# First output projection: two weight blocks kept together and taken row tile by row tile, the norm of each tile taken apart into two steps

## The chip, the cores and the metric

The kernel runs on one core of a Trainium2 chip. The metric is the device time of one execution in microseconds (us). A core has TensorE (PE in the profile) for matrix products and transposes, VectorE (DVE), ScalarE (ACT), GpSimd (POOL) and SyncE (SP), which issues most of the loads. Each engine takes its instructions strictly in the order of the program.

## The reference, cut to what matters

One decoder layer runs over a prompt of 1024 tokens and over a sample group of 8 sequences with 8 new tokens each (64 rows), with 512 past positions of each in paged caches. The model width is 1024, the inner width of the feed-forward part 2816.

```
xn  = RMSNorm(x);  z = xn @ W_in
x   = x + [ RG-LRU | gated conv | forgetting attention | differential attention ] @ W_out
x   = x + (silu(RMSNorm(x) @ W_gate) * (RMSNorm(x) @ W_up)) @ W_down
y   = RMSNorm(x)
```

The change touches the end of the second line and the norm that begins the third, for the first half of the prompt (512 tokens, four row tiles of 128).

## The kernel before, in words

**Products.** All inputs are float32. A factor is held as a high part (`whi`, `xTh`) in a reduced float32 format and a low part (`wlo`, `xTl`, what is left over), and a product takes three matmuls: L94, L95 and L96. A weight block is loaded into one of **three `raw` buffers** (L310, L312). ACT then makes the high part of a quarter of it (L325) and DVE or GpSimd the low part (L326); the pairs stand in a **ring of eight**, so two blocks' worth of them can be there at a time. `W.load_to` and `W.split_to` run ahead of the products while `W.ahead` is on.

**First output projection** (`w_out_items(0, ...)`, L1593). W_out is cut into four column blocks n of 256. For each block, four row tiles t of 128 tokens are taken, each with 24 matmuls of 256 columns (8 blocks of the inner dimension by three). DVE adds the result to the residual `acc[t]` (L1608). All of block 0 comes first, then 1, 2 and 3.

**Second norm** (`norm2_items`, `norm_T`). For each tile: ACT squares and sums `acc[t]` (L430) into a scratch tile; `rsqrt_col` makes the reciprocal root in eight small operations on DVE (L432, L122 to L125); DVE scales by it and by the gain (L442) into the scratch tile; PE transposes it in eight steps (L449); ACT and DVE make the high and low parts (L451, L452). The scratch tile and the gain come from the same ring of three `raw` buffers as the weight blocks. The transposed tiles are new (`xT_tiles`).

**Attention of the samples** (`sample_items`). For each group of sequences: transposes of the gathered key pages (`spgk`, L1421), scores (L1436), a softmax on DVE and ACT (L1469 to L1479), transposes of the probabilities (L1490, L1493), products with the new and the gathered values (L1504, L1509), and a selection (L1519, L1523). After the last group follow a norm on DVE (L1539 to L1545) and two transposes (L1548).

**What sets the order.** The program is a list of items with estimated costs; `merge(a, b, frac)` interleaves two lists so that b is used up when `frac` of a's cost is. A list scheduler then orders each engine's instructions. Before, the output projection is merged with the first 60% (`P3_SMP`) of the sample attention, the four norms with the rest. Then come the loads of the prompt's second attention pass (`att1_open`) and the gate and up products of the feed-forward part, merged with that attention (scores at L1057). The first gate/up block is taken in two halves of 256 tokens (a gate half needs norm tiles 0 and 1, the other 2 and 3), the later ones over all 512.

Of the kernel before, what the change touches and what calls it, by code (L numbers as in the profile page):

```python
# [12 lines left out]
OP = mybir.AluOpType  # L13
# [29 lines left out]
P3_SMP = 0.6  # L43
# [5 lines left out]
NP_F = 8  # L49
# [4 lines left out]
WO_HEAD = 24  # L54
# [10 lines left out]
def hybrid_step(ctx, tc, I, C, O):  # L65
    nc = tc.nc
# [308 lines left out]
    W = WStream()  # L375
    widx = {}
# [46 lines left out]
    def gload(pool, src, eng=None):  # L423
        g = big(pool, "ng", 1)
        (eng or nc.sync).dma_start(g, dap(src, 0, [[0, 128], [1, D]]))
        return g
# [7 lines left out]
        (rsqrt_act if act else rsqrt_col)(y[:R], ms[:R], nrm, nm + "rs")  # L434
        return y

    st_x = {}

    def norm_T(pool, x, gb, R, xh, xl, c0, act=False):
        xs = big(pool, "nxs", 2)[:R]  # L440
        y = rstd_of(x, xs, R, "n", act)
        st_x["x"] = nc.vector.scalar_tensor_tensor(xs, x, y[:R], gb[:R], op0=OP.mult, op1=OP.mult)  # L442
        kn = 512 // R
        for kk in range(8 // kn):
            pt = bank("t")
            pv = pt.rearrange("p (k r) -> p k r", r=R)
            for i in range(kn):
                k = kk * kn + i
                nc.tensor.transpose(pv[:, i, :], xs[:, k * 128:(k + 1) * 128], ident[:R, :R])  # L449
            ks = slice(kk * kn, (kk + 1) * kn)  # L450
            nc.scalar.activation(xh[:, ks, c0:c0 + R], pv, AF.Copy)  # L451
            nc.vector.tensor_tensor(xl[:, ks, c0:c0 + R], pv, xh[:, ks, c0:c0 + R].bitcast(F32), op=OP.subtract)  # L452
        if R == 64:
            nc.vector.tensor_copy(xh[:, :, c0 + 64:c0 + 128], xl[:, :, c0:c0 + 64].bitcast(F32))

    def xT_tiles(pool, smp):
        xh = pool.tile([128, 8, 640 if smp else 512], F32R, name="xTh")
# [794 lines left out]
    def merge(a, b, frac=1.0):  # L1252

        r = []
        ca = sum(x[0] for x in a) * frac or 1
        cb = sum(x[0] for x in b) or 1
        i = j = 0
        xa = xb = 0.0
        while i < len(a) or j < len(b):
            if j >= len(b) or (i < len(a) and xa / ca <= xb / cb):  # L1260
                xa += a[i][0]
                r.append(a[i])
                i += 1
            else:
                xb += b[j][0]
                r.append(b[j])
                j += 1
        return r
# [322 lines left out]
                nc.sync.dma_start(xl[:, k, HALF:576].bitcast(F32), yD[k][0][1][:, HALF:576])  # L1591

    def w_out_items(hf, e):  # L1593
        items = []

        def f(n, t, c, kind):
            def mm(pt, k):
                wh, wl = wget("wo", hf, n)(k)
                yh, yl = e["xh"], e["xl"]
                if kind == "p":  # L1600
                    mm3(pt[:, :256], yh[:, k, c], yl[:, k, c], wh, wl, k == 0, k == 7)
                else:
                    nc.tensor.matmul(pt[:, :256], lhsT=yh[:, k, c], rhs=wh, start=k == 0, stop=False)
                    nc.tensor.matmul(pt[:, :256], lhsT=yh[:, k, c], rhs=wl, start=False, stop=k == 7)

            def end(pt):
                a = e["acc"][t][:, n * 256:(n + 1) * 256]
                nc.vector.tensor_tensor(a, a, pt[:, :256], op=OP.add)  # L1608
            r = []
            contract(r, (24 if kind == "p" else 16) * 256 * 0.417, ("wo", hf, n), 4, mm, end)  # L1610
            return r
        for n in range(4):
            r = [f(n, t, c, kind) for t, c, kind in tok_tiles(hf)]
            if hf == 0 and n == 0:
                items += sum((x[:3] for x in r[:3]), []) + sum((x[3:] for x in r[:3]), [])
                r = r[3:]
            items += sum(r, [])
        return items

    def fold_sample(a):  # L1620
        tm = wp.tile([128, RAWW], F32, name="raw", bufs=3)[:64, :D]
# [251 lines left out]
    def norm2_items(hf, e):  # L1873
# [14 lines left out]
            return g  # L1888
        return [(900, f(t)) for t in range(4 + hf)]

    def final_items(hf, e):
        st = {}

        def ends(ch):

            def g():
                a = e["acc"][3]
                if ch == 0:
                    o = st[3] = st["o"][:, 3]
                    ss = st["ss", 3] = nrm.tile([128, 4], F32, name="fs4")  # L1900
                    nc.scalar.activation(o[:, 0:512], a[:, 0:512], AF.Square, scale=256.0, accum_out=ss[:, 0:1])
                    nc.vector.tensor_scalar(ss[:, 3:4], ss[:, 0:1], EPS * 2.0 ** 26, None, op0=OP.add)
                    nc.vector.tensor_tensor(o[:, 0:512], a[:, 0:512], st["g"][:, 0:512], op=OP.mult)
                    return
                o, ss = st[3], st["ss", 3]
                w = slice(256 + ch * 256, 512 + ch * 256)
                nc.scalar.activation(o[:, w], a[:, w], AF.Square, scale=256.0, accum_out=ss[:, ch:ch + 1])
                if ch == 1:
                    return
                ms = nrm.tile([128, 1], F32, name="fms", bufs=5)  # L1910
                nc.vector.tensor_scalar(ms, ss[:, 3:4], ss[:, 1:2], ss[:, 2:3], op0=OP.add, op1=OP.add)
                y = nrm.tile([128, 1], F32, name="fry", bufs=5)
                rsqrt_act(y, ms, nrm, "frs")
                dst = O["y_prompt"][0, hf * HALF + 384:hf * HALF + 512, :]
                nc.vector.scalar_tensor_tensor(o[:, 512:], a[:, 512:], y, st["g"][:, 512:], op0=OP.mult, op1=OP.mult)
                nc.scalar.activation(o[:, 0:512], o[:, 0:512], AF.Copy, scale=y)
                nc.scalar.dma_start(dst[:, 0:512], o[:, 0:512])
                nc.sync.dma_start(dst[:, 512:], o[:, 512:])
            return g

        def f(t, ch):
            if hf and t == 3:
                return ends(ch)
            R = 128 if t < 4 else 64

            def square(a, h):
                nc.scalar.activation(st[t][:, h * 512:(h + 1) * 512], a[:R, h * 512:(h + 1) * 512], AF.Square,
                                     scale=256.0, accum_out=st["ss", t][:R, h:h + 1])

            def g():  # L1930
                a = e["acc"][t]
                if "g" not in st:
                    st["g"] = gload(None, I["norm_final_g"])
                    st["o"] = E2[0]["xp"].tile([128, 4, D], F32, name="fo", tag="xTh")
                    st["s"] = E2[0]["xp"].tile([128, 4, D], F32, name="fos", tag="xTl")
                if ch == 0:
                    st[t] = (st["o"][:, t] if t < 4 else st["s"][:, 0])[:R]
                    st["ss", t] = nrm.tile([128, 2], F32, name="fss", bufs=5)
                    if t < 4:
                        square(a, 0)  # L1940
                    return
                if t == 4:
                    fold_sample(a)
                    square(a, 0)
                square(a, 1)
                o, ss = st[t], st["ss", t]
                ms = nrm.tile([128, 1], F32, name="fms", bufs=5)
                nc.vector.tensor_scalar(ms[:R], ss[:R, 0:1], ss[:R, 1:2], EPS * 2.0 ** 26, op0=OP.add, op1=OP.add)
                y = nrm.tile([128, 1], F32, name="fry", bufs=5)
                (rsqrt_act if hf and t in (0, 1, 2, 3) else rsqrt_col)(y[:R], ms[:R], nrm, "frs")  # L1950
                pool = t in (FIN_POOL[:2] if hf else FIN_POOL)
                if pool:
                    nc.scalar.activation(o, a[:R], AF.Copy, scale=y[:R])
                    nc.gpsimd.tensor_tensor(o, o, st["g"][:R], op=OP.mult)
                dst = O["y_prompt"][0, hf * HALF + t * 128:hf * HALF + (t + 1) * 128, :] if t < 4 else \
                    O["y_sample"].rearrange("s t d -> (s t) d")
                if not pool:
                    nc.vector.scalar_tensor_tensor(o, a[:R], y[:R], st["g"][:R], op0=OP.mult, op1=OP.mult)
                nc.sync.dma_start(dst, o)
            return g  # L1960
        return f
# [12 lines left out]
    def do(f):  # L1974
        return [(0, f)]

    E1 = [{}, {}]
    E2 = [{}, {}]
# [118 lines left out]
    prog = do(head)  # L2097
# [5 lines left out]
    n = len(lg0)  # L2103
# [7 lines left out]
    k = len(G0["lg1"] + G0["fq"] + G0["fk"]) + len(F0["lg"])  # L2111
# [10 lines left out]
    SM_ITEMS = sample_items(SM)  # L2122
# [3 lines left out]
    n = NP_F  # L2126
# [11 lines left out]
    head, mid = block_split(ffn0, [("gu", 0, P3B - 1)])  # L2138
    mid, tail = block_split(mid, [("gu", 0, P4_SPLIT)])
    smp = SM_ITEMS[3:]  # L2140
    k = int(len(smp) * P3_SMP)
    wo = w_out_items(0, E2[0])
    prog += SM_ITEMS[:3] + wo[:WO_HEAD] + merge(wo[WO_HEAD:], smp[:k]) + merge(norm2_items(0, E2[0]), smp[k:]) + do(att1_open)
    prog += merge(head, att_items(A1, 1), P3_FRAC)
    prog += do(p3_b) + mid + do(p4_open) + w_out_items(1, E2[1])
    prog += merge(tail, norm2_items(1, E2[1]), 0.8)
# [92 lines left out]
```

## Time and profile before

| | |
|---|---|
| median of 3 runs | 1379.26 us (1373.75 to 1382.87) |
| profiled execution, its own time | 1379.24 us |
| span of the profiled execution | 1376.9 us |
| mean granted clock of TensorE | 0.991 of 2.4 GHz |
| last output-projection product of the stage | starts at 436.73 us |
| first gate product | starts at 453.57 us |

All positions are microseconds from the start of the span. "Busy" is the time in which an engine has an instruction running; the granted clock is 1.00 at 2.4 GHz and 0.50 at 1.2 GHz. A row of the timeline may stand for several equal instructions in a row: "x4" with a busy time for all four. A float32 product outside L94 to L96 shows as two records for each matmul. Behind a row, in brackets, stands the idle time of the engine ahead of it and what ended it.

### The profile page before, as it was taken

The page shows a single profiled execution, that of the slowest core. Times are in us where ns is not written, and L with a number is a line of the kernel's source. Part 1 is how long each engine was busy: PE and PEld are TensorE (multiplying, and loading weights), DVE is VectorE, ACT ScalarE, POOL GpSimd, SP SyncE. Part 2 cuts the span into 40 slices and gives each one's busy share as a digit, 9 for nine tenths or more (in the row PEclk, how much of TensorE's full clock was granted, in tenths as well). Part 3 has the DMA queues.
Part 4 walks back from the last instruction along what each step waited for, and adds up shares of the span by engine and source line. Part 5 has one row for each costly group of instructions (what it writes and reads, how often), then busy time and mean ns, then how long its engine had stood idle before and what let it go on. Part 6 is the DMA issues. An engine that isn't in the chain of part 4 may idle for free.

```text
span 1376.9 us, 23077 instructions
## 1 busy us (share of the span) xinstructions
PE 1345.7 (98%) x8477; PEld 1181.9 (86%) x8477; DVE 1060.9 (77%) x2699; ACT 675.6 (49%) x1326; POOL 126.7 (9%) x154
## 2 busy tenths in 40 slices
PE   9899998999999999999999999999999999999997
PEld 7799896878876688888888999997999999999996
DVE  6676377788556568899979988547998888888885
ACT  6575466756333258755544444324533444444454
POOL 3001012302243011000000000000200000000001
PEclk9999999999999999999999999999999999999999
DMA  8566438666994366444236433611624333333311
GB/s 260 175 194 205 132 125 266 205 201 222 343 333 142 108 216 217 139 138 123 77 115 196 125 92 93 191 47 62 197 63 123 93 92 92 93 92 93 93 47 69
DMA packets 202866, 202.65 MB, mean 147 GB/s; under 512 B 16529, under 2 KB 165549, under 8 KB 202626
## 3 DMA queue, kind: packets, MB, share of 16 engines
q1 hardware_dynamic: 189568, 168.60, 40.2%
q0 software_dynamic: 7328, 25.11, 5.0%
q10 hardware_dynamic: 5858, 7.47, 1.5%
q8 instruction: 67, 1.10, 0.3%
q14 instruction: 45, 0.37, 0.1%
HBM read 170.56 MB, written 32.29 MB: 147 GB/s over the span
## 4 chain that ended last, share of the span: by engine, by line
PE 81%; DVE 6%; ACT 6%; DMA 5%; issue 1%; SPq 0%; ACTq 0%; POOL 0%; DVEq 0%
PE pb_mm L94 11%; PE pb_mm L95 10%; PE pb_mm L96 10%; PE pb_mm L1743 8%; PE pb_s L1743 5%; PE pb_t L1743 5%; PE pb_t L94 3%; PE pb_t L95 2%; PE pb_t L96 2%; PE pb_o L1743 2%; PE pb_s L96 2%; PE pb_s L95 2%; PE pb_s L94 2%; PE pb_o L1161 2%; PE pb_t L1141 2%; DMA raw<-in_w_in_dram 2%
## 5 line engine op out<-in xcount | busy, mean ns | idle before, releaser
L325 ACT ACTIVATE whi<-raw 128x512 fp32r<-128x512 f32 (+1 forms) x409 | 251.8, 629 | 350.9 <-PE pb_mm L96 75.5
L326 DVE TENSOR_TENSOR wlo<-raw,whi 128x512 fp32r<-128x512 f32 (+1 forms) x405 | 275.8, 692 | 70.5 <-ACT whi L325 60.6
L94 PE MATMUL pb_mm<-xTh,whi 128*128 128x512 f32 (+2 forms) x536 | 192.3, 359 | 0.8 <-ACT whi L325 0.8
L95 PE MATMUL pb_mm<-xTl,whi 128*128 128x512 f32 (+2 forms) x536 | 191.1, 357 | 0.3 <-DVE xTl L452 0.3
L96 PE MATMUL pb_mm<-xTh,wlo 128*128 128x512 f32 (+2 forms) x536 | 190.6, 356 | 0.3 <-DVE wlo L326 0.3
L96 PEld LDWEIGHTS pb_mm<-xTh,wlo 128*128 128x128 f32 x536 | 101.0, 188 | 13.7 <-issue 1.6
L94 PEld LDWEIGHTS pb_mm<-xTh,whi 128*128 128x128 f32 x536 | 101.3, 189 | 12.7 <-ACT whi L325 1.1
L95 PEld LDWEIGHTS pb_mm<-xTl,whi 128*128 128x128 f32 x536 | 101.2, 189 | 10.8 <-DVE xTl L452 0.5
L94 PE MATMUL pb_mm<-whi,xTh 128*128 128x256 f32 (+1 forms) x312 | 91.1, 292 | 0.0
L1099 ACT ACTIVATE aP<-aP,anm 128x128 f32<-128x128 f32 (+7 forms) x96 | 74.0, 772 | 34.5 <-DVE anm L1097 32.2
L95 PE MATMUL pb_mm<-wlo,xTh 128*128 128x256 f32 (+1 forms) x312 | 88.3, 283 | 0.2 <-POOL wlo L326 0.2
L96 PE MATMUL pb_mm<-whi,xTl 128*128 128x256 f32 (+1 forms) x312 | 88.2, 283 | 0.0
L1829 DVE TENSOR_TENSOR acc<-acc,pb_mm 128x512 f32<-128x512 f32 (+1 forms) x95 | 64.4, 678 | 15.1 <-PE pb_mm L96 13.2
L94 PE MATMUL pb_mm<-whi,hTh 128*128 128x512 f32 (+1 forms) x179 | 70.7, 395 | 0.3 <-ACT hTh L1803 0.3
L96 PE MATMUL pb_mm<-whi,hTl 128*128 128x512 f32 (+1 forms) x179 | 70.6, 394 | 0.0
L95 PE MATMUL pb_mm<-wlo,hTh 128*128 128x512 f32 (+1 forms) x179 | 70.3, 393 | 0.0
L94 PEld LDWEIGHTS pb_mm<-whi,xTh 128*128 128x128 f32 x312 | 59.0, 189 | 5.0 <-issue 4.2
L95 PEld LDWEIGHTS pb_mm<-wlo,xTh 128*128 128x128 f32 x312 | 59.0, 189 | 0.8 <-POOL wlo L326 0.4
L96 PEld LDWEIGHTS pb_mm<-whi,xTl 128*128 128x128 f32 x312 | 58.9, 189 | 0.6 <-issue 0.4
L1743 PE MATMUL pb_mm<-xTh,whi 128*128 128x288 f32 (+1 forms) x184 | 53.7, 292 | 0.0
L1743 PE MATMUL pb_mm<-xTh,wlo 128*128 128x288 f32 (+1 forms) x184 | 53.6, 292 | 0.0
L1743 PE MATMUL pb_mm<-xTl,whi 128*128 128x288 f32 (+1 forms) x184 | 53.6, 292 | 0.0
(623 smaller groups left out, 3778.3 us busy)
## 6 DMA issues: line engine op xcount, KB each, us to landing
raw<-in_w_gate_dram SPq DMA_DIRECT2D x44, 512.0 KB
raw<-in_w_up_dram SPq DMA_DIRECT2D x44, 512.0 KB
raw<-in_w_down_dram SPq DMA_DIRECT2D x22, 1024.0 KB
raw<-in_w_in_dram SPq DMA_DIRECT2D x12, 1024.0 KB
raw<-in_w_in_dram SPq DMA_DIRECT2D x16, 512.0 KB
raw<-in_w_out_dram SPq DMA_DIRECT2D x8, 1024.0 KB
akt<-fkD SPq DMA_DIRECT2D x24, 256.0 KB
akt<-dkD SPq DMA_DIRECT2D x48, 128.0 KB
```

Of the source, the lines that this page charges most:

```text
L94: kp(nc.tensor.matmul(out, lhsT=lh, rhs=rh, start=first, stop=False))
L95: kp(nc.tensor.matmul(out, lhsT=lh, rhs=rl, start=False, stop=False))
L96: kp(nc.tensor.matmul(out, lhsT=ll, rhs=rh, start=False, stop=last))
L325: i1 = nc.scalar.activation(hi, s, AF.Copy)
L326: i2 = (nc.gpsimd if pool else nc.vector).tensor_tensor(lo, s, hi.bitcast(F32), op=OP.subtract)
L1099: nc.scalar.activation(dst[:, :ln], dst[:, :ln], AF.Exp, bias=nmx, accum_out=sm)
L1141: nc.tensor.transpose(pt[:, o:o + 128], P[ti][:, kb * 128:(kb + 1) * 128], ident)
L1161: nc.tensor.matmul(po[:, q0:q0 + n], lhsT=v[:, kb, :], rhs=a[:, o:o + n], start=kb == 0 and i == 0, stop=kb >= nkb - 2 and i == 1, skip_gr ...
L1743: nc.tensor.matmul(pt, lhsT=w[:, k], rhs=x[:, k], start=first and k == 0 and i == 0, stop=k == 3 and i == 2, skip_group_check=True)
L1829: nc.vector.tensor_tensor(a, a, pt, op=OP.add)
```

## The change

Weight blocks 0 and 1 of the output projection stay as they were. Blocks 2 and 3 are now taken together, row tile by row tile: for each tile the products of block 2, then of block 3, then the first step of its norm (`norm_a`: square and sum, reciprocal root, scale). The second step of the tile before (`norm_b`: transposes and copies) follows. Splitting ahead is off in this part; the four quarters of the first gate/up block are split in it by hand, between the last tile's products of block 2 and of block 3. All of the sample attention is merged with this list. The transposed tiles are written into the same `xh`, `xl` that held the projection's input. The second step of tile 3 comes after the first 16 items of the gate and up products (the first half of the first block).

```
-    def norm_T(pool, x, gb, R, xh, xl, c0, act=False):
+    def norm_a(pool, x, gb, R, act=False):
         xs = big(pool, "nxs", 2)[:R]
         y = rstd_of(x, xs, R, "n", act)
...
+        return xs
+    def norm_b(xs, R, xh, xl, c0):
...
-            items += sum(r, [])
-        return items
+            if hf == 0 and n >= 2:
+                late.append(r)
+            else:
+                items += sum(r, [])
+        return (items, late) if hf == 0 else items
...
-    k = int(len(smp) * P3_SMP)
-    wo = w_out_items(0, E2[0])
-    prog += SM_ITEMS[:3] + wo[:WO_HEAD] + merge(wo[WO_HEAD:], smp[:k]) + merge(norm2_items(0, E2[0]), smp[k:]) + do(att1_open)
+    wo, (w2, w3) = w_out_items(0, E2[0])
+    nrm2 = norm2_steps(E2[0])
+
+    def split_next():
+        i = widx["gu", 0, 0]
+        W.split_to(i, 4)
+
+    rows = do(lambda: setattr(W, "ahead", False))
+    for t in range(4):
+        rows += w2[t] + (do(split_next) if t == 3 else []) + w3[t] + do(nrm2[t][0])
+        if t:
+            rows.append((430, nrm2[t - 1][1]))
+    prog += SM_ITEMS[:3] + wo[:WO_HEAD] + merge(wo[WO_HEAD:] + rows, smp) + do(lambda: setattr(W, "ahead", True))
+    prog += head[:2 * NP_F] + [(430, nrm2[3][1])] + do(att1_open)
+    head = head[2 * NP_F:]
     prog += merge(head, att_items(A1, 1), P3_FRAC)
```

The added lines move what follows: L449, L451, L452 of before are L452, L454, L455 after, and the lines of the sample attention stand six further down (L1421 is L1427, L1436 is L1442, L1548 is L1554).

On **ACT**, around the first square of the second norm (L430; `acc0` is the residual of tile 0; the `whi` rows ahead of it in the first piece are the high parts of the first gate/up block), before:

```order
L325 ACTIVATE whi_5516<-raw_5225 128x512
L325 ACTIVATE whi_5520<-raw_5225 128x512
L325 ACTIVATE whi_5524<-raw_5225 128x512
L325 ACTIVATE whi_5528<-raw_5225 128x512
L1423 ACTIVATE skT_5540<-pb_t_5541 128x512
L430 ACTIVATE raw_5768,nss_5769<-acc0_4829 128x1024
```

The same place after (`raw_5273` is the first gate/up block, `raw_5391` the second, `acc1` the residual of tile 1):

```order
L325 ACTIVATE whi_5982<-raw_5273 128x512
L325 ACTIVATE whi_5986<-raw_5273 128x512
L325 ACTIVATE whi_5990<-raw_5273 128x512
L325 ACTIVATE whi_5994<-raw_5273 128x512
L325 ACTIVATE whi_6126<-raw_5391 128x512
L325 ACTIVATE whi_6130<-raw_5391 128x512
L430 ACTIVATE raw_5485,nss_5486<-acc0_4829 128x1024
L325 ACTIVATE whi_6134<-raw_5391 128x512
L325 ACTIVATE whi_6138<-raw_5391 128x512
L430 ACTIVATE raw_5699,nss_5700<-acc1_4831 128x1024
```

Square of tile 0 now stands behind six high parts in one piece, two of them of the second gate/up block, and Square of tile 1 behind the other two.

On **PE**, from the last output-projection product (L96) on, before:

```order
L95 MATMUL pb_mm<-wlo,xTh 128x256
L96 MATMUL pb_mm<-whi,xTl 128x256
L1523 MATMUL pb_t<-som,sc 64x256
L449 MATMUL pb_t<-ident,raw 128x128 x8
L1436 MATMUL pb_t<-zS_dk_87,sqbd_5428 32x64 x2
L1436 MATMUL pb_t<-zS_dk_88,sqbd_5434 32x64 x2
L1421 MATMUL pb_t<-ident,spgk 128x128 x8
L1436 MATMUL pb_s<-skT,sqbd_5428 32x512
L1490 MATMUL pb_t<-ident,sP 128x128 x4
L1493 MATMUL pb_t<-ident,sP 64x128
L449 MATMUL pb_t<-ident,raw 128x128 x3
L1504 MATMUL pb_o<-vS_d,sPT 128x256
```

and after, from the same product:

```order
L95 MATMUL pb_mm<-wlo,xTh 128x256
L96 MATMUL pb_mm<-whi,xTl 128x256
L452 MATMUL pb_t<-ident,raw 128x128 x8
L1496 MATMUL pb_t<-ident,sP 128x128 x4
L1499 MATMUL pb_t<-ident,sP 64x128
L1427 MATMUL pb_t<-ident,spgk 128x128 x3
L1510 MATMUL pb_o<-vS_d,sPT 128x256
L1515 MATMUL pb_o<-spgv,sPT 64x256 x8
L1427 MATMUL pb_t<-ident,spgk 128x128 x5
L1442 MATMUL pb_s<-skT,sqbd_5360 32x512
L1442 MATMUL pb_s<-skT,sqbd_5366 32x512
L1529 MATMUL pb_t<-som,sc 64x256
```

The transposes of tile 0 (`raw`) stand right behind the product in both; after, one group's value products (L1515) come first, and a second group's follow before the first gate product.

On **PE**, around the final transposes of the sample attention (`syd`), before:

```order
L96 MATMUL pb_mm<-xTh,wlo 128x512
L94 MATMUL pb_mm<-xTh,whi 128x512
L1548 MATMUL pb_t<-ident,syd 128x64 x2
L95 MATMUL pb_mm<-xTl,whi 128x512
```

and after:

```order
L1515 MATMUL pb_o<-spgv,sPT 64x256 x8
L452 MATMUL pb_t<-ident,raw 128x128 x5
L1529 MATMUL pb_t<-som,sc 64x256
L1554 MATMUL pb_t<-ident,syd 128x64 x2
L452 MATMUL pb_t<-ident,raw 128x128 x8
L94 MATMUL pb_mm<-xTh,whi 128x256 x2
```

They stood 44 gate and up products behind the last selection (L1523); now they follow it at once (L1529, L1554), and the transposes of tile 3 and the second token half of the first gate/up block come behind them.

## Rows read from the trace of the kernel before

**Rows 1.** The page: busy time, share of the span, instructions of the engines

```profile
PE 1345.7 (98%) x8477; PEld 1181.9 (86%) x8477; DVE 1060.9 (77%) x2699; ACT 675.6 (49%) x1326; POOL 126.7 (9%) x154
```

**Rows 2.** By stretch: us; PE, PEld, DVE, ACT, POOL busy; PEclk; DMA

```profile
437.00:454.00 17.00, 14.36 (x62) 7.70 (x61) 11.65 (x35) 5.97 (x12) 0.94 (x1) 0.61 0.03 11
...
525.00:550.00 25.00, 24.99 (x152) 20.90 (x150) 22.17 (x81) 21.25 (x38) 5.08 (x10) 1.00 0.72 219
```

**Rows 3.** By stretch, in 2 us slices (columns as above)

```profile
440.00:442.00 2.00, 1.52 (x8) 1.45 (x8) 1.73 (x9) 2.00 (x5) 0.00 (x0) 0.66 0.00 0
442.00:444.00 2.00, 1.27 (x4) 0.18 (x2) 1.63 (x10) 1.02 (x3) 0.00 (x0) 0.50 0.00 0
...
454.00:456.00 2.00, 1.98 (x15) 1.40 (x16) 1.42 (x5) 1.90 (x4) 0.00 (x0) 0.92 0.71 213
```

**Rows 4.** Timeline of PE: start, us, engine, line, operation, output<-inputs, shapes, count

```profile
436.73 0.28 PE L96 MATMUL pb_mm<-whi,xTl 128*128 128x256 f32 x1
...
437.51 0.66 PE L449 MATMUL pb_t<-ident,raw 128*128 128x128 f32 x4
...
448.79 3.68 PE L1509 MATMUL pb_o<-spgv,sPT 128*64 128x256 f32 x16
...
453.57 0.80 PE L94 MATMUL pb_mm<-xTh,whi 128*128 128x256 f32 x2
```

**Rows 5.** Timeline of ACT: high parts of the first gate/up block, and two squares

```profile
414.43 1.34 ACT L325 ACTIVATE whi<-raw 128x512 fp32r<-128x512 f32 x2 [2.77 <-PE pb_mm L96]
...
420.65 1.06 ACT L430 ACTIVATE raw<-acc 128x1024 f32<-128x1024 f32 x1 [3.73 <-DVE acc L1608]
...
439.60 1.05 ACT L430 ACTIVATE raw<-acc 128x1024 f32<-128x1024 f32 x1
```

**Rows 6.** Timeline of DVE: a low part, and the scale of a norm

```profile
437.01 0.69 DVE L326 TENSOR_TENSOR wlo<-raw,whi 128x512 fp32r<-128x512 f32 x1 [0.87 <-ACT whi L325]
...
444.23 1.28 DVE L442 SCALAR_TENSOR_TENSOR raw<-acc,nry,raw 128x1024 f32<-128x1024 f32 x1
```

**Rows 7.** PE in 437 to 454 by group: count | busy, mean ns | idle before

```profile
L1509 PE MATMUL pb_o<-spgv,sPT 128*64 128x256 f32 x16 | 3.7, 641 | 0.0
...
L1436 PE MATMUL pb_s<-skT,sqbd 128*32 128x512 f32 x2 | 1.9, 1060 | 0.7 <-ACT skT L1423 0.7
L1421 PE MATMUL pb_t<-ident,spgk 128*128 128x128 f32 x8 | 1.9, 411 | 0.6 <-DVE xTl L452 0.6
L1504 PE MATMUL pb_o<-vS_d,sPT 64*128 64x256 f32 x2 | 1.2, 712 | 0.0
L1490 PE MATMUL pb_t<-ident,sP 128*128 128x128 f32 x4 | 1.1, 435 | 0.0
```

**Rows 8.** Timeline of PE at full clock, from 470 us on (columns as above)

```profile
470.50 0.64 PE L1421 MATMUL pb_t<-ident,spgk 128*128 128x128 f32 x4
...
475.53 0.38 PE L94 MATMUL pb_mm<-xTh,whi 128*128 128x256 f32 x1
...
485.88 0.28 PE L96 MATMUL pb_mm<-xTh,wlo 128*128 128x256 f32 x1
486.00 0.40 PE L94 MATMUL pb_mm<-xTh,whi 128*128 128x512 f32 x1
...
490.53 0.33 PE L1548 MATMUL pb_t<-ident,syd 64*128 64x64 f32 x2
```

**Rows 9.** Timeline of DVE: from the last selection to the final norm's root

```profile
483.03 0.41 DVE L1529 TENSOR_TENSOR syd<-syd,pb_t 64x256 f32<-64x256 f32 x1
...
488.41 0.15 DVE L105 SCALAR_TENSOR_TENSOR srs_z<-srs_z,sms 64x4 f32<-64x4 f32 x1
488.60 0.15 DVE L106 SCALAR_TENSOR_TENSOR sry<-srs_z,sry 64x4 f32<-64x4 f32 x1
```

**Rows 10.** Waits of SP's queue in 350 to 500: total, times, longest

```profile
SPq L310 <- DVE raw L442: 59.9, 1, 59.9
```

**Rows 11.** Timeline of PE: the first score of the prompt's second attention pass

```profile
502.04 0.33 PE L1057 MATMUL pb_s<-akt,aqt 128*128 128x384 f32 x1
```

More of the change, by code (lines that the diff above doesn't have):

```diff
@@ L435, in rstd_of @@
         return y
-    st_x = {}
-    def norm_T(pool, x, gb, R, xh, xl, c0, act=False):
+    def norm_a(pool, x, gb, R, act=False):
         xs = big(pool, "nxs", 2)[:R]
         y = rstd_of(x, xs, R, "n", act)
-        st_x["x"] = nc.vector.scalar_tensor_tensor(xs, x, y[:R], gb[:R], op0=OP.mult, op1=OP.mult)
+        nc.vector.scalar_tensor_tensor(xs, x, y[:R], gb[:R], op0=OP.mult, op1=OP.mult)
+        return xs
+    def norm_b(xs, R, xh, xl, c0):
         kn = 512 // R
@@ L454, in norm_T @@
             nc.vector.tensor_copy(xh[:, :, c0 + 64:c0 + 128], xl[:, :, c0:c0 + 64].bitcast(F32))
+    def norm_T(pool, x, gb, R, xh, xl, c0, act=False):
+        norm_b(norm_a(pool, x, gb, R, act), R, xh, xl, c0)
     def xT_tiles(pool, smp):
@@ L1593, in w_out_items @@
     def w_out_items(hf, e):
-        items = []
+        items, late = [], []
         def f(n, t, c, kind):
@@ L1889, in norm2_items, with norm2_steps, a, f @@
         return [(900, f(t)) for t in range(4 + hf)]
+    def norm2_steps(e):
+        st = {}
+        def a(t):
+            def f():
+                if t == 0:
+                    st["g"] = gload(None, I["norm_ffn_g"])
+                st[t] = norm_a(None, e["acc"][t], st["g"], 128)
+            return f
+        def b(t):
+            def f():
+                norm_b(st[t], 128, e["xh"], e["xl"], t * 128)
+            return f
+        return [(a(t), b(t)) for t in range(4)]
     def final_items(hf, e):
```

## The prediction

> **What bounds the kernel now.** I read the engine table of the page first: PE is busy in 98% of the span [rows 1]. So what can be won or lost is time in which PE stands still or runs at half clock. Next the table of stretches [rows 2]. In 525 to 550 us, with the second attention pass under way, PE is busy for 24.99 of 25 us at full clock: what comes behind cannot swallow a delay. Between 437 and 454 us it is busy for 14.36 of 17 us at a granted clock of 0.61. This is the stretch that the change rewrites. The finer table [rows 3] shows how it goes: PE is busy for 1.52 and 1.27 us of two slices of 2 us, the clock falls to 0.50 (the 1.2 GHz level), and only in 454 to 456 does it come back. The loss is 2.6 us of standing still and about 6 us of half clock (some 12 us at 0.50): 8 to 9 us together, 0.6% of the time. A better order of this stretch can give back no more.
>
> The timeline shows why PE loosens there. T is the end of the last product of the first output projection, 437.0 us. The first gate product, which needs norm tiles 0 and 1, starts at 453.57, 16.6 us later [rows 4]. Tile 0 adds little to that wait: its Square ran at 420.65, behind the high parts of the first gate/up block (the last two at 414.43) and 16 us ahead of T [rows 5], so its transposes start 0.5 us behind T [rows 4]. Tile 1 and one group of the sample attention fill the rest.
>
> **What the change does to that stretch.** It is written to take each tile's norm behind that tile's products. The order of ACT shows something else. The scratch tile of a norm comes out of the ring of three `raw` buffers. When the norms are due, the gain holds one and the first two gate/up blocks hold the others, so tile 0 gets its scratch only when all four quarters of the first gate/up block are split. A split needs a pair out of a ring of eight. Before, it took the pairs of weight block 2, done long before T. Now blocks 2 and 3 hold all eight to the last row tile: the first gate/up block waits for the last tile's products of block 2, the second for those of block 3. ACT's rows say the same: six high parts ahead of Square of tile 0, two more ahead of tile 1. No norm is earlier than before; tile 0's moves from 16 us ahead of T to the very end.
>
> **A: from T to the transposes of tile 0.** The last products run at 0.12 us each (485.88 and 486.00, [rows 8]), a quarter of a block, six of them, in 0.71. The second quarter of block 3 is done at T - 1.4; its high part takes 0.67 (half of 1.34), so Square starts at about T - 0.8 and ends 1.05 later [rows 5], its sum at about T + 0.4. Then come eight small operations on DVE. The small ones of another root follow each other by 0.19 us (488.41, 488.60, [rows 9]); 1.9 with hand-overs is my estimate. Two low parts of 0.69 lie among them, and the scale takes 1.28 [rows 6]. That makes T + 5.0, with a hand-over to PE 5.2. PE's next row behind the last product is these transposes, so it stands still for all of it; before it was 0.5.
>
> **B: from there to the first gate product.** The order has there, besides 16 transposes of tiles 0 and 1, two groups of sample attention (before one). At half clock, by the groups of before [rows 7]: two value sets of 3.7 and two of 1.2; two sets of four probability transposes of 1.1; 16 norm transposes of the same shape, 4.4; 16 page transposes, 3.8; four wide scores of 0.95 (1.9 is two records, one matmul is two); for one selection, eight small scores and two single transposes 2.4, an estimate from those shapes. Sum 26.6. Before, half clock lasted some 12 us [rows 3]; I take the same, and the other 14.6 at half of that, 7.3. PE stood still for 2.6 us with one group [rows 2]; with two I take 4.5. First gate product at T + 5.2 + 12 + 7.3 + 4.5 = T + 29.0, against T + 16.6: **+12.4**. Bounds: +9 if DVE and ACT are ahead of PE while it is slow, +15.9 if the clock stays low throughout (5.2 + 26.6 + 0.7).
>
> A rule weighs against the change here. The Trainium skill, page "TensorE: Matmul & The Clock Gate", section "Part 4: PE-mode transpose", says that full clock does not engage for transposes, because they do not count as a busy array in the same way. By it the clock would not return before the gate products, and B would end on its upper bound. The trace does not contradict it: 0.50 lasted through page and norm transposes, and 0.92 came behind the value products from 448.79 and with the gate products from 453.57 [rows 3, 4].
>
> **C: from the first gate product to the second token half.** Before 453.57 to 475.53 [rows 4, 8], 22.0 us. The second half needs tiles 2 and 3. At full clock the new order has 48 products there (5.7), 8 page and 16 norm transposes at 0.16 (3.9, [rows 8]), one group's values, probability transposes and scores at half of [rows 7] (1.9 + 0.6 + 0.6 + 1.5), two selections, small scores and the last two transposes (2.2, estimated): 16.4. And there is a new stop. The final transposes of the sample attention (L1548) stand right behind its last selection, with nothing between; behind a selection DVE does a square, a sum and a three-step root, which ran from 483.03 until PE's transposes at 490.53 [rows 8, 9], under 44 gate and up products. Its operations alone, four of 0.41 and twelve at 0.19 [rows 9], are worth 3.9 us, with hand-overs some 4.6. 16.4 + 4.6 + 1.5 of smaller waits = 22.5: **+0.5**. Bounds -2 (DVE is ahead, the stop is 2) and +4 (gate work stands in DVE's queue ahead of the root).
>
> **D: to the end of the first gate/up block.** Before 475.53 to 486.0 [rows 8], 10.5 us, of which 5.7 were products and the rest attention. Now 5.7, and behind a stop of 4.6 us the clock falls once more: I take +4. With the 0.3 that L1548 no longer takes later, **-0.3**; without the second fall -4.3.
>
> **Moved ahead of T:** 8 page transposes (1.3) and a score, **+1.7** with hand-overs. The write in place costs nothing, since the same copies go to another tile; nor does the head of 16 items, the same products elsewhere.
>
> **What is queued behind.** SP's load of the third gate/up block waits for tile 3's scale, 59.9 us before [rows 10], and still does. Behind it stand the first loads of the second attention pass, whose first score came at 502.04, 16 us behind the first gate/up block [rows 8, 11]. Now only 11 wide products stand between that block and the score. A wait of 0 to 3 us is possible; I take 0, because a slow second half covers it.
>
> **Sum:** 12.4 + 0.5 - 0.3 + 1.7 = +14.3 on the profiled execution's 1379.24 (median 1379.26, span 1376.9): **1393.5 us**. Measurements of this kernel, three from 1373.75 to 1382.87, tell about 1% from no change: 13.8 us, up to 1393.05. My sum lies just past that border.
>
> **The rivals.** *Lighter:* no second fall of the clock, and a shorter stop in C; 4 and 2.5 off the sum, 1387. For it: the gate work ahead of the stop is dense. [...]
> *Heavier:* half clock to the first gate product (+3.5), 12 us of it again behind the stop (+2), attention loads late (+3): 1402. For it: the transposes that fill B.
> *Not slower:* the norms do leave the path. Were Square of tile 0 to start in the third row tile, its transposes would stand ready at T and PE would never loosen; the 8 to 9 us come back, 1371. It decides at one point: a `raw` buffer free for the scratch before T - 5. Against: the rows of ACT.
> *No effect:* the attention groups only change places and PE's stops come out as before: 1380. Against: stop A stands in the order.
>
> **How the numbers follow.** Forecast (1388 to 1400) 0.53, lighter (1382 to 1388) 0.20, heavier (1400 to 1405) 0.14, no effect 0.08, not slower 0.05. Past 1393.05 lie about 0.6 of the forecast and all of the heavier case, 0.32 + 0.14: slower 0.46. Faster by over 1% takes more than the stretch holds: 0.03. Within 1%: 0.51. Range 1381 to 1402: it leaves out no effect, not slower and half of the heavier case.
>
> **What would show it.** Right: a stop of PE of 4 to 6 us right behind the last product, ended by tile 0's scale; Square of tile 0 within 2 us of T; a longer stretch at 0.50; a stop of 4 to 5 us ahead of the final transposes. Wrong: Squares of tiles 0 to 2 well ahead of T, or a clock of 1.00 throughout; then A and B fall out of the sum.

## The result and the profile after

The changed kernel takes 1396.6 us (median of 4 runs, 1396.0 to 1398.6) against 1378.0 (median of 4 runs of the kernel before). The ratio is 1.0143, with a 95% interval of 1.0119 to 1.0167 (the two medians alone give 1.0135): slower by over 1%. The forecast was 1393.5 us, in a range of 1381 to 1402. The profiled execution took 1396.58 us, with a span of 1394.8, 17.9 us longer than that of before.

The table of stretches of the kernel after (stretch, its length, then busy time of PE, PEld, DVE, ACT, POOL, granted clock, DMA share, GB/s), cut at the places that the prediction spoke of:

```profile
437.00:443.00 6.00, 6.00 (x51) 5.81 (x50) 4.62 (x8) 4.53 (x7) 0.00 (x0) 1.00 0.01 1
443.00:471.00 28.00, 18.66 (x98) 9.88 (x98) 17.29 (x51) 7.49 (x16) 0.94 (x1) 0.82 0.07 19
471.00:494.00 23.00, 16.87 (x114) 12.10 (x115) 14.03 (x47) 5.27 (x12) 0.88 (x2) 0.89 0.30 93
494.00:501.00 7.00, 7.00 (x52) 6.74 (x52) 3.79 (x6) 3.12 (x7) 0.92 (x3) 0.87 0.82 249
```

Where PE was busy for 14.36 of 17 us [rows 2], it is now busy for 18.66 of 28, and then for 16.87 of 23. The timeline of PE shows the two stops (in brackets: idle time ahead of the row, and what ended it) and the marks between which the prediction counted:

```profile
442.73 0.28 PE L96 MATMUL pb_mm<-whi,xTl 128*128 128x256 f32 x1
447.65 1.60 PE L452 MATMUL pb_t<-ident,raw 128*128 128x128 f32 x8 [4.64 <-DVE nms L432]
...
470.85 0.51 PE L94 MATMUL pb_mm<-xTh,whi 128*128 128x256 f32 x2 [0.25 <-ACT xTh L454]
...
491.74 0.44 PE L1554 MATMUL pb_t<-ident,syd 64*128 64x64 f32 x2 [4.66 <-DVE syd L1551]
492.46 1.97 PE L452 MATMUL pb_t<-ident,raw 128*128 128x128 f32 x8 [0.27 <-DVE syt L1557]
494.26 1.22 PE L94 MATMUL pb_mm<-xTh,whi 128*128 128x256 f32 x3
...
500.96 0.39 PE L95 MATMUL pb_mm<-xTl,whi 128*128 128x512 f32 x1
```

T, the end of the last product of the output projection, is 443.0. PE then stands still for 4.64 us until the transposes of tile 0, and later for 4.66 us until the final transposes of the sample attention. Between the marks, against [rows 4, 8]:

| stretch | before | after | difference |
|---|---|---|---|
| start of the span to T | 437.0 | 443.0 | +6.0 |
| T to the first gate product | 16.6 | 27.9 | +11.3 |
| to the second token half | 22.0 | 23.4 | +1.4 |
| to the first product of the second gate/up block | 10.5 | 6.7 | -3.8 |
| to the end of the span | 890.9 | 893.8 | +2.9 |

The sum is 17.8 us, the 17.9 by which the spans differ but for rounding. The timeline of ACT shows why tile 0 is late:

```profile
438.10 4.18 ACT L325 ACTIVATE whi<-raw 128x512 fp32r<-128x512 f32 x6 [6.66 <-PE pb_mm L96]
442.19 1.04 ACT L430 ACTIVATE raw<-acc 128x1024 f32<-128x1024 f32 x1
...
443.22 1.13 ACT L325 ACTIVATE whi<-raw 128x512 fp32r<-128x512 f32 x2
445.34 1.06 ACT L430 ACTIVATE raw<-acc 128x1024 f32<-128x1024 f32 x1 [0.98 <-DVE wlo L326]
```

Before its first high part ACT waited 6.66 us for products of block 2; then come six high parts in a piece, and Square of tile 0 at 442.19, 0.8 us ahead of T, where it ran 16 us ahead of T before [rows 5].

### The profile page after: what moved, and what is told of

The parts are those of the page before. It is cut to its first block, busy times and chain, and to the rows that moved or that the text cites. A ratio compares the mean times of both kernels' runs of the same rounds, so it can differ in the third digit from the quotient of the medians.

```text
span 1394.8 us, 23066 instructions
## 1 busy us (share of the span) xinstructions
PE 1347.9 (97%) x8477; PEld 1181.5 (85%) x8477; DVE 1059.8 (76%) x2699; ACT 676.3 (48%) x1326; POOL 125.0 (9%) x154
## 4 chain that ended last, share of the span: by engine, by line
PE 71%; DMA 8%; issue 8%; DVE 7%; ACT 5%; SPq 1%; POOL 0%; ACTq 0%; POOLq 0%; DVEq 0%
PE pb_mm L94 8%; PE pb_mm L95 8%; PE pb_mm L96 8%; PE pb_mm L1752 7%; PE pb_s L1752 5%; PE pb_t L1752 4%; PE pb_s L95 2%; PE pb_s L94 2%; PE pb_t L94 2%; PE pb_o L1752 2%; PE pb_s L96 2%; PE pb_t L96 2%; PE pb_t L95 2%; PE pb_o L1167 2%; DVE wlo L326 1%
## 5 line engine op out<-in xcount | busy, mean ns | idle before, releaser
L96 PE MATMUL pb_mm<-xTh,wlo 128*128 128x512 f32 (+2 forms) x536 | 190.6, 356 | 0.3 <-DVE wlo L326 0.3
L96 PEld LDWEIGHTS pb_mm<-xTh,wlo 128*128 128x128 f32 x536 | 101.1, 189 | 12.0 <-DVE wlo L326 0.5
L96 PE MATMUL pb_mm<-whi,xTl 128*128 128x256 f32 (+1 forms) x312 | 88.5, 284 | 0.0
L96 PE MATMUL pb_mm<-whi,hTl 128*128 128x512 f32 (+1 forms) x179 | 70.5, 394 | 0.0
L96 PEld LDWEIGHTS pb_mm<-whi,xTl 128*128 128x128 f32 x312 | 59.0, 189 | 0.3 <-DVE xTl L572 0.2
L1152 DVE TENSOR_TENSOR aAl<-pb_t,aAh 128x512 fp32r<-128x512 f32 (+1 forms) x80 | 49.2, 632 | 10.4 <-ACT aAh L1151 9.1
L1151 ACT ACTIVATE aAh<-pb_t 128x512 fp32r<-128x512 f32 (+1 forms) x80 | 42.3, 550 | 29.9 <-PE pb_t L1147 26.6
```

Source lines behind the costliest of these rows:

```text
L96: kp(nc.tensor.matmul(out, lhsT=ll, rhs=rh, start=False, stop=last))
L1151: nc.scalar.activation(ah[:, :o], pt[:, :o], AF.Copy)
L1152: nc.vector.tensor_tensor(al[:, :o], pt[:, :o], ah[:, :o].bitcast(F32), op=OP.subtract)
```

## The experiments

**The scratch buffer.** One edit on the changed kernel keeps the second gate/up block out of the ring of three raw buffers while blocks 2 and 3 are taken:

```
         def load_to(self, n):
-            while self.nl < min(n, len(self.specs)):
+            while self.nl < min(n, len(self.specs), self.lim):
...
+    def hold():
+        W.ahead = False
+        W.lim = widx["gu", 0, 0] + 1
+    def free():
+        W.ahead = True
+        W.lim = 9999
-    rows = do(lambda: setattr(W, "ahead", False))
+    rows = do(hold)
...
-... merge(wo[WO_HEAD:] + rows, smp) + do(lambda: setattr(W, "ahead", True))
+... merge(wo[WO_HEAD:] + rows, smp) + do(free)
```

> The changed kernel with one difference: the second gate/up block is not loaded while blocks 2 and 3 of the output projection are taken row tile by row tile, so that one of the three raw buffers is free for the norms' scratch. Theory (the scratch buffer holds the norm back): Square of tile 0 runs 10 us or more ahead of the last output-projection product T, the stop of 4.65 us behind T is gone, the granted clock stays at 1.00 there, T to the first gate product falls from 27.9 us to under 15, and the time is 1380 to 1387 us. Rival (the norm is late for another reason, such as the write in place into tiles that the projection still reads): the order may change, but the stop stays, and the time is 1392 to 1398 us. Second rival (the late load costs as much as it frees): the first row tiles improve, PE then waits for the second gate/up block, 1390 to 1397 us.

Measured: 1381.8 us, 14.9 less than the changed kernel; ratio to before 1.002 (1.0000 to 1.0041). The profiled execution took 1377.8 us, the second fastest of ten. Its timelines of ACT (first two rows) and PE:

```profile
409.46 1.06 ACT L431 ACTIVATE raw<-acc 128x1024 f32<-128x1024 f32 x1 [0.83 <-DVE acc L1615]
...
428.11 0.60 ACT L455 ACTIVATE xTh<-pb_t 128x512 fp32r<-128x512 f32 x1 [0.75 <-PE pb_t L453]
...
457.04 0.28 PE L96 MATMUL pb_mm<-whi,xTl 128*128 128x256 f32 x1
457.15 0.29 PE L94 MATMUL pb_mm<-xTh,whi 128*128 128x256 f32 x1
...
474.18 0.44 PE L1555 MATMUL pb_t<-ident,syd 64*128 64x64 f32 x2 [6.35 <-DVE syd L1552]
```

Square of tile 0 waits only for the sum of its own tile and runs at 409.46. The last product of the projection (457.04) is followed by the first gate product after 0.11 us, where 27.9 us lay between. So this one load, kept out of the ring, lets the norms move ahead of T, and the stop and the half clock behind T go with it. T itself comes 14.3 us later, at 457.3, because attention work that stood behind it now stands ahead of it; the first gate product comes 13.7 us earlier than in the changed kernel. The first rival fell: the high part of tile 0 is written into the projection's own `xTh` at 428.11, 29 us ahead of T, so the write in place does not hold the norm. The second did not come either: from 410 to 500 us PE waits for no weight block. The later stop, ahead of the final transposes (L1555 here), stays and grows from 4.66 to 6.35 us.

**The final transposes.** One edit on the changed kernel moves the last item of the sample attention, its norm and transposes, behind the next eight items of the gate/up list:

```
-    smp = SM_ITEMS[3:]
+    smp = SM_ITEMS[3:-1]
...
-    prog += head[:2 * NP_F] + [(430, nrm2[3][1])] + do(att1_open)
-    head = head[2 * NP_F:]
+    prog += head[:2 * NP_F] + [(430, nrm2[3][1])] + head[2 * NP_F:3 * NP_F] + SM_ITEMS[-1:] + do(att1_open)
+    head = head[3 * NP_F:]
```

> The changed kernel with one difference: the final norm and transposes of the sample attention come 8 items later (behind the gate product of the second block), so that PE has the second token half under the DVE root. Theory (the stop of 4.66 us ahead of these transposes is on the path, with a short fall of the clock behind it): the stop is gone and the time falls by 4.7 to 8 us, to 1389 to 1392 us. Rival (the first loads of the prompt's second attention pass wait for the sample attention's memory, so the stop only moves to the first score): a wait of 3 to 5 us at the first score, time 1394 to 1398 us.

Measured: 1389.4 us, 7.2 less than the changed kernel; ratio to before 1.0085 (1.0056 to 1.0115). In its timeline of PE the transposes of tile 3 now come without the final ones ahead of them, at full clock, and the final ones follow without a stop:

```profile
488.68 1.21 PE L452 MATMUL pb_t<-ident,raw 128*128 128x128 f32 x8
...
496.03 0.31 PE L1554 MATMUL pb_t<-ident,syd 64*128 64x64 f32 x2
```

The stop is worth 4.7, the slower transposes behind it 0.8 (1.97 against 1.21) and the slower second token half 1.0 (6.7 against 48 products of 0.118, 5.7). That is 6.5 of the 7.2. The rival, a stop that moves to the first score of the attention, did not come.

**Both edits.**

> Both edits of the two runs before together. Theory: the two gains add up, PE has neither of the two stops, and the time is 1372 to 1381 us, at or under the kernel before. Rival (the stops hide one another, or the loads of the second attention pass become the next wait): 1385 to 1392 us.

> The kernel with both edits once more, beside the slower pace on the same chip. Expected 1373 to 1376 us; PE's idle time between 360 and 410 us between 1 and 3.5 us if it varies from execution to execution, at 2.9 us if it is fixed by the order.

Measured: 1374.4 and 1374.3 us, ratios 0.998 (0.9959 to 1.0001) and 0.9975 (0.9955 to 0.9996). The two gains, 14.9 and 7.2, add up to 22.1; together they bring 22.2. The runs of these kernels spread over 3 to 9 us, so that the gains add up is shown, and the agreement to 0.1 us is luck. In the two stretches behind 443 us of the first profile, PE is busy throughout and the clock stands at 1.00:

```profile
443.00:471.00 28.00, 27.98 (x208) 21.27 (x207) 19.64 (x56) 9.66 (x19) 0.00 (x0) 1.00 0.07 20
471.00:500.00 29.00, 28.73 (x154) 23.93 (x154) 20.32 (x60) 13.71 (x27) 3.99 (x8) 1.00 0.97 279
```

This is the order that the change was written for, and it is worth some 3 to 4 us against the kernel before (the intervals end at 1.0001 and 0.9996, so this gain is just at the edge of what is shown), less than the 8 to 9 that stood still or ran slow in [rows 2, 3]. A part of the rest shows in the stretch from 360 to 410 us, ahead of T. In both edits' first profile (its clock fell once there, to 0.97 on average), in their second, in the kernel after, and in the kernel before:

```profile
360.00:410.00 50.00, 47.07 (x412) 38.93 (x414) 21.50 (x51) 14.76 (x30) 20.79 (x26) 0.97 0.95 323
```

```profile
360.00:410.00 50.00, 46.63 (x416) 39.60 (x415) 24.30 (x58) 16.03 (x32) 22.67 (x27) 1.00 0.98 329
```

```profile
360.00:410.00 50.00, 46.40 (x405) 38.52 (x404) 21.96 (x53) 14.77 (x30) 22.50 (x27) 1.00 1.03 346
```

```profile
360.00:410.00 50.00, 48.58 (x441) 42.39 (x440) 23.07 (x57) 15.12 (x31) 22.37 (x27) 1.00 1.01 346
```

PE is idle there for 2.9, 3.4 and 3.6 us, in the kernel before for 1.4. With both edits that is 1.5 to 2.0 us more than before; where the other 3 us or so are lost is not located. The samples' pace is higher, because all of their attention is merged with the projection, and the next runs ask whether that is the reason.

**The pace in the kernel before.** One constant of the kernel before, P3_SMP from 0.6 to 1.0, gives it the pace of the changed kernel.

> The kernel before with one constant changed, P3_SMP 1.0 instead of 0.6: all of the sample attention is merged with the output projection, at the pace that it has in the changed kernel; blocks, norms and scratch are as before. Theory on the late T of the changed kernel (the faster pace makes PE wait for the gathered pages): PE's idle time between 360 and 410 us rises by 2 to 3 us, with waits for the page gathers, as in the changed kernel. The norms then have little cover: a longer idle stretch behind T, but less work there; time 1376 to 1388 us. Rival (the pace costs nothing, T was late because blocks 2 and 3 are interleaved): no waits for gathers, the idle time between 360 and 410 us as before, time 1374 to 1382 us.

Measured: 1383.9 us, ratio 1.0041 (1.0017 to 1.0064). The same two stretches:

```profile
360.00:410.00 50.00, 45.85 (x402) 38.36 (x402) 23.39 (x57) 15.42 (x31) 23.05 (x27) 1.00 1.03 347
443.00:471.00 28.00, 21.37 (x165) 15.38 (x163) 17.21 (x59) 6.17 (x12) 0.00 (x0) 0.95 0.15 48
```

PE's idle time from 360 to 410 rises from 1.4 to 4.2 us, with blocks and norms as before; 2.9 of it are waits for gathered pages. These are single executions, though, and the kernel with the later weight block, which has the pace of the changed kernel, was idle there for only 1.3 us:

```profile
360.00:410.00 50.00, 48.74 (x444) 39.51 (x443) 23.02 (x53) 15.89 (x32) 22.95 (x28) 1.00 0.94 321
```

Most of the 6.6 us idle in the later stretch of the kernel before at the higher pace is the stop of 5.4 us ahead of the final transposes, which have no products in front of them here either; its timeline of PE:

```profile
471.31 0.47 PE L1548 MATMUL pb_t<-ident,syd 64*128 64x64 f32 x2 [5.38 <-DVE syd L1545]
```

**A slower pace.** Here the first half of the first gate/up block joins the list with which the samples are merged, once with both edits and once in the changed kernel alone:

```
-    prog += ... merge(wo[WO_HEAD:] + rows, smp) + do(free)
-    prog += head[:2 * NP_F] + [(430, nrm2[3][1])] ...
+    prog += ... merge(wo[WO_HEAD:] + rows + do(free) + head[:2 * NP_F], smp)
+    prog += [(430, nrm2[3][1])] ...
```

> The kernel with both edits (second gate/up block loaded later, final norm of the samples later) and a third: the first half of the first gate/up block stands in the list with which the sample attention is merged, so that the samples' pace in the output projection is about a fifth slower. Theory (the faster pace makes PE wait for gathered pages between 360 and 410 us): its idle time there, 2.9 us with both edits, falls to 1 to 2 us, with less waiting for page gathers; the rest stays, and the time falls by 1 to 2 us against both edits, to 1371 to 1374 us. Rival (those waits come from the weight loads beside the gathers, whatever the pace): idle time there stays at 2.5 to 4 us, time 1373 to 1377 us.

> The changed kernel with the slower pace alone (the first half of the first gate/up block in the list with which the sample attention is merged). Theory: idle time of PE between 360 and 410 us falls from 3.6 us to 1.5 to 2.5, T comes 2 to 4 us earlier because less sample work stands ahead of it, but that work comes behind T, where the stop by the norm stays: time 1393 to 1396 us. Rival (the late T was a loss of its own and comes back in full): 1390 to 1392 us.

Both expectations failed, theory and rival alike: 1382.4 us (ratio 1.0039, 1.0022 to 1.0055), 8 more than both edits; and 1403.6 us (1.0209, 1.0174 to 1.0243), 7 more than the changed kernel. With both edits the idle time from 360 to 410 falls to 1.95 us as expected (48.05 busy); in the changed kernel it does not fall, 3.8 us in place of 3.6:

```profile
360.00:410.00 50.00, 46.19 (x410) 39.44 (x409) 22.47 (x55) 15.15 (x32) 21.91 (x26) 1.00 1.01 341
```

So a slower pace does not reliably take these waits away, as a higher one did not always bring them. What is put off comes back elsewhere. The timeline of PE of the first:

```profile
467.88 0.28 PE L96 MATMUL pb_mm<-xTh,wlo 128*128 128x256 f32 x1
470.59 0.66 PE L1497 MATMUL pb_t<-ident,sP 128*128 128x128 f32 x4 [2.42 <-DVE sP L1486]
...
472.22 0.70 PE L1511 MATMUL pb_o<-vS_d,sPT 64*128 64x256 f32 x2 [0.86 <-DVE sPT L1501]
```

and the waits of PE of the second (total, times, longest):

```profile
PE pb_t L1496 <- DVE sP L1485: 4.9, 2, 3.1
PE pb_t L452 <- DVE nms L432: 4.6, 1, 4.6
PE pb_t L1554 <- DVE syd L1551: 4.1, 1, 4.1
```

The last attention group now stands behind the last product that could cover its softmax. With both edits PE is idle for 6.2 us from 443 to 500, against 0.3 without the slower pace: 3.8 us are waits of this group, and 2.2 are a wait of the second attention pass's first score for its keys. So a group that is left over behind the dense products cost more here than the waits of the higher pace.

**The weight block beside the gathers.** With both edits, the load of the first gate/up block is put behind the gain and the samples' tables:

```
     def hold():
         W.ahead = False
-        W.lim = widx["gu", 0, 0] + 1
+        W.lim = widx["gu", 0, 0]
...
+        if t == 0:
+            rows += do(lambda: setattr(W, "lim", widx["gu", 0, 0] + 1)) + do(lambda: W.load_to(widx["gu", 0, 0] + 1))
```

> The kernel with both edits and one more: the load of the first gate/up block (1 MB) is issued behind the gain and the sample attention's tables instead of ahead of them; the order on PE is nearly the same, the samples' pace is the same. Theory (PE's idle time between 360 and 410 us, 2.9 to 3.4 us with both edits, is waiting for data on DMA queues that are full there, so the weight block beside them is the cause): idle time there falls to 1 to 2 us and the time by 1 to 2 us, to 1371 to 1374 us. Rival (it is the samples' pace alone): idle time there stays at 2.5 to 3.5 us, time 1373 to 1377 us.

Measured: 1372.9 us, ratio 0.9963 (0.9942 to 0.9984). The time came out as the theory had it, its reason did not: PE's idle time from 360 to 410 rose to 4.2 us. What ends the waits there changes from execution to execution. Both edits, first profile, second profile, and this kernel:

```profile
PE pb_t L1428 <- DMA spgk<-in_cache_fox_k_dram,idx: 2.0, 1, 2.0
PE pb_t L1428 <- ACT skT L1430: 0.5, 1, 0.5
```

```profile
PE pb_mm L94 <- DVE acc L1615: 1.5, 1, 1.5
PE pb_t L1428 <- ACT skT L1430: 1.4, 1, 1.4
```

```profile
PE pb_mm L94 <- DVE acc L1615: 2.2, 1, 2.2
PE pb_t L1428 <- ACT skT L1430: 1.6, 1, 1.6
```

The longest wait is once for a page gather and twice for the addition into a residual tile (L1615); the next is each time for the copy of the transposed keys (`skT`). The first two pieces belong to the same kernel in two executions and differ. So the cause of these waits is not settled, neither by the pace nor by the weight block. The kernel is the fastest of the study, but its interval overlaps that of both edits, so a gain of its own is not shown.

## Why the prediction was right, point by point

The path was right; that the total came so near is in part luck, as the terms show.

**The bound** was read rightly: no stretch gave the delay back, and the order that the change was meant to be gained less than the 8 to 9 us named as the limit.

**The mechanism** held. Square of tile 0 was forecast at T - 0.8 and came 0.8 us ahead of T, behind six high parts. That the scratch buffer is what holds it is shown by the first experiment, which keeps one load out of that ring and leaves the rest of the program's list as it is. The other half of the reasoning, the ring of eight pairs that makes the high parts late, agrees with ACT's wait of 6.66 us for products of block 2, but was not tried by itself. The rival "not slower" named the same point as the one that decides; with it changed, and with the second stop gone, its side came true, with a smaller gain.

**A**, the stop behind T: 5.2 us forecast, 4.64 measured. **B**, to the first gate product: T + 29.0 forecast, T + 27.9 measured, +11.3 in place of +12.4. PE stood still behind the transposes of tile 0 for 4.7 us, 4.5 forecast. The half clock lasted some 10 us in place of 12, but its length did not decide: with the final transposes moved, whose order is the same up to here, the granted clock over the stretch was 0.76 in place of 0.82, which makes some 13 us at 0.50 (an estimate, 0.24 of 28 us by 0.5), and the first gate product still came some 28 us behind T:

```profile
443.00:471.00 28.00, 19.25 (x102) 10.69 (x102) 18.13 (x51) 8.05 (x16) 0.94 (x1) 0.76 0.06 20
```

The terms printed for B add up to 26.4, not 26.6, which is 0.1 us at half of it. In the kernel after, the clock fell once PE had stood still from 443.0 to 447.65, and came back behind the first group of value products:

```profile
446.00:448.00 2.00, 0.35 (x3) 0.38 (x4) 1.87 (x5) 0.49 (x2) 0.00 (x0) 1.00 0.00 0
448.00:450.00 2.00, 1.25 (x7) 0.85 (x5) 1.79 (x7) 1.31 (x3) 0.00 (x0) 0.51 0.00 0
...
456.00:458.00 2.00, 2.00 (x12) 1.18 (x10) 0.17 (x1) 0.00 (x0) 0.00 (x0) 0.50 0.00 0
458.00:460.00 2.00, 1.75 (x11) 0.67 (x9) 1.09 (x2) 0.60 (x1) 0.94 (x1) 0.93 0.00 0
```

By the rule on transposes in the Trainium skill's page "TensorE: Matmul & The Clock Gate" (section "Part 4: PE-mode transpose") the clock would have stayed low to the gate products at 470.85. It came back some 12 us ahead of them. The value products just before the rise are no transposes, so the rule itself is neither shown nor refuted; the case worked out from it fell.

**C**, to the second token half: the stop ahead of the final transposes was forecast at 4.6 us and measured at 4.66; the stretch came to +1.4 in place of +0.5. The eight transposes behind the stop ran at half clock, 1.97 us against 1.21, which is 0.8 of the difference. Of its terms, the 1.5 for scores has no row: half of the 1.9 in [rows 7] is 1.0.

**D** was mis-sized, -0.3 forecast and -3.8 measured. A part is a slip: its own terms make 5.7 + 4 - 10.5 - 0.3 = -1.1. With this and the slip in B, the forecast would have been 1392.6 us, just inside the 1% border of 1393.05. The rest is the size of the half clock. The clock did fall a second time:

```profile
488.00:490.00 2.00, 0.00 (x0) 0.00 (x0) 1.79 (x9) 0.31 (x1) 0.00 (x0) 0.75 0.85 348
490.00:492.00 2.00, 0.26 (x2) 0.28 (x2) 1.35 (x8) 0.00 (x0) 0.00 (x0) 0.50 0.00 0
492.00:494.00 2.00, 1.73 (x9) 1.55 (x8) 0.47 (x2) 0.65 (x2) 0.88 (x2) 0.50 0.07 16
494.00:496.00 2.00, 2.00 (x10) 1.74 (x10) 1.38 (x2) 0.95 (x3) 0.37 (x3) 0.55 0.13 33
496.00:498.00 2.00, 2.00 (x20) 2.00 (x19) 0.43 (x1) 0.63 (x1) 0.54 (x1) 1.00 1.02 295
```

But of the some 6.8 us at 0.50 that these rows make, 2.7 lay in the stop itself and 2.5 between its end and the second half, most of them under transposes. The second half took 6.7 us for 5.7 us of products: 1.0, where I had put 4. Behind the stop the fall cost 1.8 us in all, with the 0.8 in C.

**The step that failed** is "moved ahead of T", +1.7 forecast and +6.0 measured. The stretch up to T, from the same point of the program (0.7 us earlier in the kernel after, since small differences lie ahead of it), before and after:

```profile
340.73:437.02 96.29, 94.78 (x759) 78.84 (x759) 51.95 (x131) 29.36 (x56) 37.11 (x44) 1.00 0.87 300
```

```profile
340.00:443.02 103.02, 99.32 (x778) 80.49 (x777) 51.61 (x129) 29.95 (x57) 35.67 (x44) 1.00 0.84 282
```

It grew by 6.7 us: 4.5 of PE's busy time, which I had counted too low, and 2.2 of waiting, which I had not counted at all. PE has 19 more records there: eight page transposes and two of a wide score, which I had named, and one of a selection and eight small scores, which I had not. Their groups grew by 3.3 us; the other 1.2 lie in instructions that stand ahead of T in both kernels. The waiting lies in the stretch from 360 to 410 us, and its cause stays open: the higher pace brought such waits into the kernel before (1.4 to 4.2 us), but the later weight block had 1.3 at that pace and the changed kernel 3.8 at the slower one.

**What comes behind** was taken as 0. The first score of the attention waited 0.3 us for its keys, inside the 0 to 3 named. But the rest of the program took 2.9 us more. Most of it lies in the stretch from 560 to 1000 us, before and after:

```profile
560.00:1000.00 440.00, 438.99 (x2645) 384.96 (x2644) 363.74 (x874) 208.22 (x390) 14.14 (x7) 1.00 0.41 122
```

```profile
560.00:1000.00 440.00, 437.02 (x2597) 378.90 (x2596) 358.08 (x885) 212.83 (x398) 9.25 (x8) 1.00 0.40 119
```

PE is idle there for 3.0 us, before for 1.0, with the later weight block for 2.0, with the final transposes moved for 0.5, in the changed kernel at the slower pace for 2.2. The three kernels in which the attention's list begins right behind the first half block have the most; whether that is the cause was not tried by itself.

So the sum met two errors of size with opposite signs: 4.3 too little ahead of T, 3.5 too much in D. With 0.2 too much in B and C together and the 2.9 behind, 4.3 - 3.5 - 0.2 + 2.9 = 3.5 us, the step from +14.3 to +17.8. Had the errors not had opposite signs, the sum would have missed by much more. The chances split at the 1% border, 0.51 within it and 0.46 slower; the measured ratio lies beyond it.

## What to carry to other kernels

When steps are brought forward, look up what buffers they take, and who holds those at the new place: here a block loaded ahead held the last free one of three raw buffers, and one load less ahead gave 14.9 of the 18.6 us back. A short item that waits for a long DVE chain needs other products for PE while that chain runs: eight items later in the list, the final transposes came without a stop. Attention work spread over products should end before they do: here a group left over cost more than the waits of a pace that was a little too high.

## What was not expected of the hardware

The waits from 360 to 410 us end at different releasers in two executions of one kernel (a gather at 2.0 us in one, a residual addition at 1.5 in the other) while PE's idle time there stays near 3 us (2.9 and 3.4), with the DMA share at 0.95 and 0.98. And two stops of nearly the same length, 4.64 and 4.66 us, were followed by different lengths of half clock: some 10 us behind the first, under transposes, waiting attention steps and value products, and some 4 us behind the second, under ten transposes and then dense products.
